# A float32 transpose on one core: four staggered column ranges, 32 KB store packets, two load slots, no seam

## The chip, the cores and the metric

The kernel runs on 1 core of a Trainium2 chip. The metric is device time in microseconds (us), lower is better.

## The reference

```python
x = np.random.randn(8192, 8192).astype(np.float32)     # 256 MiB

def reference(x):
    return np.transpose(x)
```

The kernel reads 268.4 MB and writes 268.4 MB of device memory. No arithmetic counts; the work is moving bytes.

## The kernel before

In what follows PE is the matrix engine (PEld its weight loads), ACT and DVE are the scalar and the vector engine, SPq is the queue that issues the DMAs, and PSUM is the memory that PE writes.

The matrix is cut into two strips of 4096 columns. A step loads a *chunk*: 128 rows of one strip, 16 KB per SBUF partition, 2 MB in all. PE transposes the 32 blocks of 128x128 against an identity matrix into PSUM, ACT and DVE copy them into *regions* in SBUF, and a region is stored when it has collected a *window* of 8 chunks. A region holds a *range* of 4 blocks (512 columns of the input, which are 512 rows of the output) by 8 chunks, so each stored output row is 8x128 floats, 4 KB long.

The eight ranges close their windows at successive steps, so one 2 MB store is issued at each step. This needs short windows (1 to 7 chunks, so rows of 512 B to 3.5 KB) at the start and the end of each strip.

```python
    S = 32; B = 4; W = 8; NR = S // B; NIN = 3; NREG = 9; NPS = 8     # one line each in the kernel
    ...
        for t, (s, c) in enumerate(chunks):               # 2 strips x 64 chunks
            nc.tensor.wait_ge(s_ld[t % NIN], 16 * (t // NIN + 1))
            closing = []
            for q in [(c + k) % NR for k in range(NR)]:
                if q not in window:
                    end = min(c + (q - c) % W, CH - 1)    # windows end one step apart, and at the strip's end
                    r = free.pop(0)
                    window[q] = (c, end, r)
                    ...                                   # copier waits until region r was stored
                ...                                       # 4 transposes, 1 copy into the region
            for q, e, count in closing:
                ...
                dst = out[j0:j0 + B * P, c0 * P:c0 * P + rows]
                dst = dst.rearrange("(b q) i -> q b i", q=P)
                nc.sync.wait_ge(s_cp[e], count)
                st = wide_dma(nc, nc.sync, "qSPDynamicHW", dst, regs[r][:, :B * rows])
                ...
            if t + NIN < len(chunks):                     # the next load, behind the stores
                nc.sync.wait_ge(s_pe, n)
                load(t + NIN)
```

`wide_dma` issues a store whose source is one contiguous run per partition, so that a DMA packet reads 16 KB of one partition (4 blocks) and writes four output rows of 4 KB.

Of the kernel before, what the change touches and what calls it, by code (L numbers as in the profile page):

```python
# [1 line left out]

# [4 lines left out]


def physical(ap):


    t = ap.tensor
    dims = [list(d) for d in ap.ap]
    if len(dims) == 2:
        dims.insert(1, [dims[1][1], 1])
    return mybir.PhysicalAccessPattern(
        ap=dims,
        offset=ap.offset,
        dtype=ap.dtype,
        memref=t.name,  # L20
        memsetref=t.name + "_set",
    )


def wide_dma(nc, eng, queue, out, in_):


    return eng.add_instruction(
        mybir.InstDMACopy(
            mode="Copy",  # L30
            name=nc.get_next_instruction_name(),
            engine=eng.engine,
            ins=[physical(in_)],
            outs=[physical(out)],
            queue=queue,
        )
    )


@with_exitstack  # L40
def kernel(
    ctx: ExitStack,
    tc: tile.TileContext,
    x: bass.AP,
    out: bass.AP,
):





    nc = tc.nc
    P = 128
    N, M = x.shape
    assert x.shape == out.shape[::-1]
    dt = x.dtype

    S = 32
    B = 4
    W = 8  # L60
    NR = S // B
    NIN = 3
    NREG = 9
    NPS = 8
    CH = N // P
    J = S * P

    with tc.tile_critical():  # L68
        nc.alloc_sbuf_tensor("pad", [P, 32], dt)
        ident = nc.alloc_sbuf_tensor("ident", [P, P], dt).ap()  # L70
        ins = [nc.alloc_sbuf_tensor(f"in{k}", [P, J], dt).ap() for k in range(NIN)]
        regs = [nc.alloc_sbuf_tensor(f"reg{k}", [P, B * W * P], dt).ap() for k in range(NREG)]
        pss = [nc.alloc_psum_tensor(f"ps{k}", [P, B * P], dt).ap() for k in range(NPS)]

        s_id = nc.alloc_semaphore("s_id")
        s_ld = [nc.alloc_semaphore(f"s_ld{k}") for k in range(NIN)]
        s_st = [nc.alloc_semaphore(f"s_st{k}") for k in range(NREG)]
        s_pe = nc.alloc_semaphore("s_pe")
        s_cp = [nc.alloc_semaphore("s_cpa"), nc.alloc_semaphore("s_cpv")]

        nc.gpsimd.memset(ident, 0.0).then_inc(s_id, 1)  # L81
        nc.gpsimd.wait_ge(s_id, 1)
        nc.gpsimd.affine_select(  # L83
            out=ident,
            in_=ident,
            compare_op=mybir.AluOpType.not_equal,
            fill=1.0,
            base=0,
            pattern=[[-1, P]],
            channel_multiplier=1,  # L90
        ).then_inc(s_id, 1)
        nc.tensor.wait_ge(s_id, 2)

        chunks = [(s, c) for s in range(M // J) for c in range(CH)]

        def load(t):
            s, c = chunks[t]
            nc.sync.dma_start(
                out=ins[t % NIN], in_=x[c * P:(c + 1) * P, s * J:(s + 1) * J]
            ).then_inc(s_ld[t % NIN], 16)  # L100

        for t in range(NIN):
            load(t)

        n = 0
        copied = [0, 0]
        bank = [None] * NPS
        free = list(range(NREG))
        stored = [0] * NREG
        window = {}  # L110
        stores = 0
        for t, (s, c) in enumerate(chunks):
            nc.tensor.wait_ge(s_ld[t % NIN], 16 * (t // NIN + 1))
            closing = []
            for q in [(c + k) % NR for k in range(NR)]:
                if q not in window:

                    end = min(c + (q - c) % W, CH - 1)
                    r = free.pop(0)
                    window[q] = (c, end, r)  # L120
                    if stored[r]:
                        (nc.scalar, nc.vector)[q % 2].wait_ge(s_st[r], 16 * stored[r])
                c0, end, r = window[q]
                rows = (end - c0 + 1) * P
                view = regs[r][:, :B * rows].rearrange("p (b i) -> p b i", b=B)
                ps = pss[n % NPS]
                e = q % 2
                if bank[n % NPS] is not None:
                    nc.tensor.wait_ge(*bank[n % NPS])
                for b in range(B):  # L130
                    last = nc.tensor.transpose(  # L131
                        ps[:, b * P:(b + 1) * P],
                        ins[t % NIN][:, (q * B + b) * P:(q * B + b + 1) * P],
                        ident,
                    )
                last.then_inc(s_pe, 1)
                n += 1
                o = view[:, :, (c - c0) * P:(c - c0 + 1) * P]
                i = ps.rearrange("p (b i) -> p b i", b=B)
                (nc.scalar, nc.vector)[e].wait_ge(s_pe, n)  # L140
                if e == 0:
                    cp = nc.scalar.copy(out=o, in_=i)  # L142
                else:
                    cp = nc.vector.tensor_copy(out=o, in_=i)  # L144
                cp.then_inc(s_cp[e], 1)
                copied[e] += 1
                bank[(n - 1) % NPS] = (s_cp[e], copied[e])
                if c == end:
                    closing.append((q, e, copied[e]))
            for q, e, count in closing:  # L150
                c0, end, r = window.pop(q)
                rows = (end - c0 + 1) * P
                j0 = s * J + q * B * P
                dst = out[j0:j0 + B * P, c0 * P:c0 * P + rows]
                dst = dst.rearrange("(b q) i -> q b i", q=P)
                nc.sync.wait_ge(s_cp[e], count)
                if stores:
                    st = wide_dma(nc, nc.sync, "qSPDynamicHW", dst, regs[r][:, :B * rows])
                else:
                    st = nc.sync.dma_start(  # L160
                        out=dst, in_=regs[r][:, :B * rows].rearrange("q (b i) -> q b i", b=B)
                    )
                st.then_inc(s_st[r], 16)
                stores += 1
                stored[r] += 1
                free.append(r)
            if t + NIN < len(chunks):
                nc.sync.wait_ge(s_pe, n)
                load(t + NIN)
        for r in range(NREG):  # L170
            nc.sync.wait_ge(s_st[r], 16 * stored[r])


# [1 line left out]
_INS = ['x']  # L175
_OUTS = [((8192, 8192), 'float32')]


# [23 lines left out]
```

## Time and profile before

1267.5 us (median of 3 runs, 1266.26 to 1268.18).

| | before |
|---|---|
| span of the profiled execution | 1265.1 us |
| PE / DVE / ACT busy | 57% / 28% / 24% |
| GB/s in most slices | 426 to 431 |
| load, issue to landing | 23.5 us |

Lines of the profile's page: the mean busy share of the 16 DMA engines in 40 slices of the span (tenths) and the rate; the share of the chain of waits by engine and by line; the costliest groups (busy us, mean ns of one, then idle time before them and what ended it); DMA issues with size and us from issue to landing.

```profile
DMA  9999999999999999999999999999999999999998
GB/s 380 418 428 427 428 429 428 427 428 428 426 428 429 426 428 430 429 428 428 428 417 428 428 427 428 431 429 429 429 428 428 430 428 430 429 429 429 428 428 353
...
DMA 78%; PE 20%; issue 0%; DVE 0%; ACT 0%; SPq 0%; ACTq 0%
...
L131 PE MATMUL ps<-ident,in 128*128 128x128 f32 x4096 | 722.6, 359 | 514.8 <-DMA in<-in_x_dram 499.7
...
in<-in_x_dram SPq DMA_DIRECT2D x128, 2048.0 KB, 23.5
out_dram<-reg SPq DMA_DIRECT2D x114, 2048.0 KB, 22.7
```

The DMA engines are busy all the time, the chain runs through them, and PE waits for loads. The Trainium skill, "DMA: Bandwidth & Descriptors", section "Where 436 GB/s comes from", gives 435.2 GB/s as the fabric's ceiling; this trace agrees with it as a ceiling, since the steady slices are at 428 to 429, 98.4% of it. (The same section says that for transfers between HBM, the device memory, and SBUF the memory side, at about 358 GB/s, binds. This trace, of one core, is above that, so the measurement decides.) So little is left to gain. The first, second, middle (seam) and last slices are slower.

The same in five uneven stretches (columns: stretch, its us, busy us of each engine with the number of instructions, granted PE clock, DMA share, GB/s):

```profile
0.00:70.00 70.00, 43.08 (x288) 41.69 (x288) 24.47 (x36) 22.18 (x37) 0.70 (x6) 0.88 0.98 402
70.00:590.00 520.00, 304.14 (x1696) 291.57 (x1696) 146.97 (x213) 124.18 (x212) 0.00 (x0) 0.74 1.01 428
590.00:740.00 150.00, 85.17 (x480) 79.26 (x480) 40.98 (x60) 34.85 (x60) 0.00 (x0) 0.70 1.01 426
740.00:1200.00 460.00, 268.28 (x1504) 257.14 (x1504) 130.04 (x188) 110.12 (x188) 0.00 (x0) 0.75 1.01 429
```

The fifth stretch is the rest of the span. The DMA share can pass 1 (it is 1.006 from 100 to 580 us), so the records of successive packets overlap in part.

### The profile page before, as it was taken

To read this page: it belongs to the slowest core of one execution; us is meant where nothing else is said; L and a number is where in the kernel's file an instruction comes from. 1 tells how busy PE (TensorE), PEld (TensorE's weight loads), DVE (VectorE), ACT (ScalarE), POOL (GpSimd) and SP (SyncE) were. 2 spreads that over 40 slices of the span, in tenths; PEclk is the share of its full clock that TensorE was granted. 3 is DMA by queue.
4 is the path that set the end of the run, shared out by engine and by line. 5 is a ranking of instruction groups with operands and counts; after the bars stand their busy time and mean duration, and the time that the engine had idled before them with its cause. 6 is when DMAs were issued, how large, how long until landed. Compare 5 with 4: busy or idle time off the path is not lost.

```text
span 1265.1 us, 9814 instructions
## 1 busy us (share of the span) xinstructions
PE 722.6 (57%) x4096; PEld 690.6 (55%) x4096; DVE 353.5 (28%) x512; ACT 300.7 (24%) x513; POOL 0.7 (0%) x6
## 2 busy tenths in 40 slices
PE   6555656665556555565456655656566555665651
PEld 6555645555456555564455555655455555565551
DVE  3322222322223222232133322223223222232220
ACT  3322222222222222222122222222222222222220
POOL 0000000000000000000000000000000000000000
PEclk8877686777776877768667777686867877777675
DMA  9999999999999999999999999999999999999998
GB/s 380 418 428 427 428 429 428 427 428 428 426 428 429 426 428 430 429 428 428 428 417 428 428 427 428 431 429 429 429 428 428 430 428 430 429 429 429 428 428 353
DMA packets 39308, 537.51 MB, mean 425 GB/s; under 512 B 4320, under 2 KB 4832, under 8 KB 6240
## 3 DMA queue, kind: packets, MB, share of 16 engines
q1 hardware_dynamic: 39264, 536.89, 100.0%
q8 instruction: 32, 0.52, 0.2%
q14 instruction: 12, 0.10, 0.0%
HBM read 268.44 MB, written 268.44 MB: 424 GB/s over the span
## 4 chain that ended last, share of the span: by engine, by line
DMA 78%; PE 20%; issue 0%; DVE 0%; ACT 0%; SPq 0%; ACTq 0%
DMA in<-in_x_dram 75%; PE ps L131 20%; DMA out_dram<-reg 2%; DVE reg L144 0%; ACT reg L142 0%; SPq L197 0%; SPq L68 0%; ACTq L140 0%
## 5 line engine op out<-in xcount | busy, mean ns | idle before, releaser
L131 PE MATMUL ps<-ident,in 128*128 128x128 f32 x4096 | 722.6, 359 | 514.8 <-DMA in<-in_x_dram 499.7
L131 PEld LDWEIGHTS ps<-ident,in 128*128 128x128 f32 x4096 | 690.6, 193 | 546.5 <-DMA in<-in_x_dram 520.8
L144 DVE COPY reg<-ps 128x512 f32<-128x512 f32 x512 | 353.5, 692 | 884.2 <-PE ps L131 850.8
L142 ACT COPY reg<-ps 128x512 f32<-128x512 f32 x512 | 299.4, 586 | 936.5 <-PE ps L131 902.7
L142 ACT ACT_TABLE_LOAD x1 | 1.3, 1283 | 0.9 <-SPq L68 0.9
L83 POOL TENSOR_SCALAR_AFFINE_SELECT ident<-ident 128x128 f32<-128x128 f32 x1 | 0.3, 292 | 0.2 <-POOL ident L81 0.2
L81 POOL MEMSET ident<- 128x128 f32 x1 | 0.2, 204 | 0.5 <-SPq L68 0.5
L186 POOL MEMSET const-bfloat16-1.0<- 128x1 bf16 x1 | 0.1, 101 | 0.0
L186 POOL MEMSET const-uint8-127<- 128x1 uint8 x1 | 0.1, 101 | 0.0
L186 POOL MEMSET const-float32-0.0<- 128x1 f32 x1 | 0.1, 98 | 0.2 <-issue 0.2
L186 POOL MEMSET const-float32-1.0<- 128x1 f32 x1 | 0.1, 98 | 0.0
## 6 DMA issues: line engine op xcount, KB each, us to landing
in<-in_x_dram SPq DMA_DIRECT2D x128, 2048.0 KB, 23.5
out_dram<-reg SPq DMA_DIRECT2D x114, 2048.0 KB, 22.7
out_dram<-reg SPq DMA_DIRECT2D x4, 1792.0 KB, 20.1
out_dram<-reg SPq DMA_DIRECT2D x4, 1536.0 KB, 19.2
out_dram<-reg SPq DMA_DIRECT2D x4, 1280.0 KB, 19.1
out_dram<-reg SPq DMA_DIRECT2D x4, 1024.0 KB, 17.9
out_dram<-reg SPq DMA_DIRECT2D x4, 768.0 KB, 16.3
out_dram<-reg SPq DMA_DIRECT2D x4, 512.0 KB, 13.2
```

What stands on the lines that cost most here:

```text
L81: nc.gpsimd.memset(ident, 0.0).then_inc(s_id, 1)
L83: nc.gpsimd.affine_select(out=ident, in_=ident, compare_op=mybir.AluOpType.not_equal, fill=1.0, base=0, pattern=[[-1, P]], channel_multipl ...
L131: last = nc.tensor.transpose(ps[:, b * P:(b + 1) * P], ins[t % NIN][:, (q * B + b) * P:(q * B + b + 1) * P], ident,)
L142: cp = nc.scalar.copy(out=o, in_=i)
L144: cp = nc.vector.tensor_copy(out=o, in_=i)
L186: nc = _bacc.Bacc("TRN2", target_bir_lowering=False, num_devices=1)
```

## The change

Its intent: halve the number of store packets (32 KB of SBUF each instead of 16), and remove the seam between the strips and the staircase of short windows there.

- Four ranges of 8 blocks, windows of 8 chunks, so a region is 32 KB per partition. Five regions (160 KB) leave room for two load slots instead of three.
- Range q begins 2q steps after range 0, and takes the rows of a strip round, so that it begins strip 1 while later ranges still finish strip 0. A load still is one contiguous piece of a row.
- A window that crosses the end of the rows or of the strip is stored in two or three parts. One window of 2 chunks per range opens the kernel; the last ones are 6 chunks.
- The load of two steps on is issued ahead of the stores of a step. PSUM copies are 128x1024 instead of 128x512.

```diff
-    S = 32
-    B = 4
+    B = 8
     W = 8
-    NR = S // B
-    NIN = 3
-    NREG = 9
-    NPS = 8
+    NR = 4
+    G = W // NR
+    NREG = 5
+    NPS = 4
...
+        at = [((t - G * q) // CH, q) for q in range(NR) if t >= G * q]
+        active.append(sorted(a for a in at if a[0] < NS))
...
+            while t1 + 1 < hi and t1 % W != (G * q + G - 1) % W:
+                t1 += 1
...
+                if t == t1 or (t + 1) % CH == 0 or (t + 1 - lo) % CH == 0:
+                    parts.append((a, t))
...
+    order = [("L", t) for t in range(4)]
+    order += [("S", 1), ("L", 4), ("S", 3), ("L", 5), ("L", 6), ("L", 7), ("S", 5)]
+    for t in range(6, T):
+        if t + 2 < T:
+            order.append(("L", t + 2))
+        if closing[t]:
+            order.append(("S", t))
...
+                for a, z in w["parts"]:
+                    rows = (z - a + 1) * P
...
+                    i0 = a % CH * P
+                    dst = out[j0:j0 + R, i0:i0 + rows].rearrange("(b q) i -> q b i", q=P)
...
+                    src = regs[w["reg"]][:, base:base + B * rows]
+                    if stores:
+                        st = wide_dma(nc, nc.sync, "qSPDynamicHW", dst, src)
```

More of the change, by code (lines that the diff above doesn't have):

```diff
@@ L56 @@
     dt = x.dtype
-    S = 32
-    B = 4
+    B = 8
     W = 8
-    NR = S // B
-    NIN = 3
-    NREG = 9
-    NPS = 8
+    NR = 4
+    G = W // NR
+    NREG = 5
+    NPS = 4
     CH = N // P
-    J = S * P
+    J = NR * B * P
+    NS = M // J
+    T = NS * CH + (NR - 1) * G
+    SPLIT = range(3 * G, 5 * G)
+    active = []
+    for t in range(T):
+        at = [((t - G * q) // CH, q) for q in range(NR) if t >= G * q]
+        active.append(sorted(a for a in at if a[0] < NS))
+    closing = [[] for _ in range(T)]
+    window_of = {}
+    for q in range(NR):
+        lo, hi = G * q, G * q + NS * CH
+        t0 = lo
+        while t0 < hi:
+            t1 = t0
+            while t1 + 1 < hi and t1 % W != (G * q + G - 1) % W:
+                t1 += 1
+            parts = []
+            a = t0
+            for t in range(t0, t1 + 1):
+                if t == t1 or (t + 1) % CH == 0 or (t + 1 - lo) % CH == 0:
+                    parts.append((a, t))
+                    a = t + 1
+            w = {"q": q, "t0": t0, "t1": t1, "parts": parts}
+            closing[t1].append(w)
+            for t in range(t0, t1 + 1):
+                window_of[t, q] = w
+            t0 = t1 + 1
+    EARLY = 3 * G
+    order = [("L", t) for t in range(4)]
[5 more added lines that the diff above has]
+            order.append(("S", t))
+    assert sorted(k for o, k in order if o == "L") == list(range(T))
+    assert sorted(k for o, k in order if o == "S") == [t for t in range(T) if closing[t]]
     with tc.tile_critical():
-        nc.alloc_sbuf_tensor("pad", [P, 32], dt)
         ident = nc.alloc_sbuf_tensor("ident", [P, P], dt).ap()
-        ins = [nc.alloc_sbuf_tensor(f"in{k}", [P, J], dt).ap() for k in range(NIN)]
+        ins = [nc.alloc_sbuf_tensor(f"in{k}", [P, J], dt).ap() for k in range(2)]
         regs = [nc.alloc_sbuf_tensor(f"reg{k}", [P, B * W * P], dt).ap() for k in range(NREG)]
@@ L75 @@
         s_id = nc.alloc_semaphore("s_id")
-        s_ld = [nc.alloc_semaphore(f"s_ld{k}") for k in range(NIN)]
+        s_ld = [nc.alloc_semaphore(f"s_ld{k}") for k in range(2)]
+        s_half = [nc.alloc_semaphore(f"s_half{k}") for k in range(2)]
+        s_early = [nc.alloc_semaphore(f"s_early{k}") for k in range(EARLY)]
         s_st = [nc.alloc_semaphore(f"s_st{k}") for k in range(NREG)]
@@ L79, with landed @@
         s_cp = [nc.alloc_semaphore("s_cpa"), nc.alloc_semaphore("s_cpv")]
+        copier = [nc.scalar, nc.vector]
+        R = B * P
+        home = []
+        pieces = []
+        count = {}
+        def landed(s):
+            count[s.name] = count.get(s.name, 0) + 16
+            return s, count[s.name]
+        last_use = []
+        for t in range(T):
+            n = len(active[t]) * R
+            if t < EARLY:
+                buf, off = [
+                    (ins[0], 0), (ins[0], R), (ins[0], 2 * R),
+                    (ins[1], 0), (regs[NREG - 1], 0), (regs[NREG - 1], 3 * R),
+                ][t]
+                home.append(buf[:, off:off + n])
+                pieces.append([(*landed(s_early[t]), 0, n)])
+                last_use.append(None)
+                continue
+            k = t % 2
+            home.append(ins[k][:, :n])
+            if t in SPLIT:
+                pieces.append([(*landed(s_half[k]), 0, n // 2), (*landed(s_ld[k]), n // 2, n)])
+            else:
+                pieces.append([(*landed(s_ld[k]), 0, n)])
+            last_use.append([2, 3][k] if t < EARLY + 2 else t - 2)
+        free = list(range(NREG))
+        stored = [0] * NREG
+        for t in range(T):
+            for s, q in active[t]:
+                w = window_of[t, q]
+                if w["t0"] == t:
+                    r = free.pop(0)
+                    w["reg"], w["before"] = r, stored[r]
+            for w in closing[t]:
+                stored[w["reg"]] += len(w["parts"])
+                free.append(w["reg"])
         nc.gpsimd.memset(ident, 0.0).then_inc(s_id, 1)
@@ L92 @@
         nc.tensor.wait_ge(s_id, 2)
-        chunks = [(s, c) for s in range(M // J) for c in range(CH)]
-        def load(t):
-            s, c = chunks[t]
-            nc.sync.dma_start(
-                out=ins[t % NIN], in_=x[c * P:(c + 1) * P, s * J:(s + 1) * J]
-            ).then_inc(s_ld[t % NIN], 16)
-        for t in range(NIN):
-            load(t)
         n = 0
+        done = []
         copied = [0, 0]
         bank = [None] * NPS
-        free = list(range(NREG))
-        stored = [0] * NREG
-        window = {}
-        stores = 0
-        for t, (s, c) in enumerate(chunks):
-            nc.tensor.wait_ge(s_ld[t % NIN], 16 * (t // NIN + 1))
-            closing = []
-            for q in [(c + k) % NR for k in range(NR)]:
-                if q not in window:
-                    end = min(c + (q - c) % W, CH - 1)
-                    r = free.pop(0)
-                    window[q] = (c, end, r)
-                    if stored[r]:
-                        (nc.scalar, nc.vector)[q % 2].wait_ge(s_st[r], 16 * stored[r])
-                c0, end, r = window[q]
-                rows = (end - c0 + 1) * P
-                view = regs[r][:, :B * rows].rearrange("p (b i) -> p b i", b=B)
+        for t in range(T):
+            todo = list(pieces[t])
+            for k, (s, q) in enumerate(active[t]):
+                if todo and todo[0][2] == k * R:
+                    nc.tensor.wait_ge(todo[0][0], todo[0][1])
+                    todo.pop(0)
+                w = window_of[t, q]
+                e = q % 2
                 ps = pss[n % NPS]
-                e = q % 2
                 if bank[n % NPS] is not None:
@@ L132 @@
                         ps[:, b * P:(b + 1) * P],
-                        ins[t % NIN][:, (q * B + b) * P:(q * B + b + 1) * P],
+                        home[t][:, k * R + b * P:k * R + (b + 1) * P],
                         ident,
@@ L137 @@
                 n += 1
-                o = view[:, :, (c - c0) * P:(c - c0 + 1) * P]
+                if w["t0"] == t and w["before"]:
+                    copier[e].wait_ge(s_st[w["reg"]], 16 * w["before"])
+                copier[e].wait_ge(s_pe, n)
+                a, z = next(p for p in w["parts"] if p[0] <= t <= p[1])
+                base = (a - w["t0"]) * R
+                o = regs[w["reg"]][:, base:base + (z - a + 1) * R]
+                o = o.rearrange("p (b i) -> p b i", b=B)[:, :, (t - a) * P:(t - a + 1) * P]
                 i = ps.rearrange("p (b i) -> p b i", b=B)
-                (nc.scalar, nc.vector)[e].wait_ge(s_pe, n)
                 if e == 0:
@@ L147 @@
                 bank[(n - 1) % NPS] = (s_cp[e], copied[e])
-                if c == end:
-                    closing.append((q, e, copied[e]))
-            for q, e, count in closing:
-                c0, end, r = window.pop(q)
-                rows = (end - c0 + 1) * P
-                j0 = s * J + q * B * P
-                dst = out[j0:j0 + B * P, c0 * P:c0 * P + rows]
-                dst = dst.rearrange("(b q) i -> q b i", q=P)
-                nc.sync.wait_ge(s_cp[e], count)
-                if stores:
-                    st = wide_dma(nc, nc.sync, "qSPDynamicHW", dst, regs[r][:, :B * rows])
-                else:
-                    st = nc.sync.dma_start(
-                        out=dst, in_=regs[r][:, :B * rows].rearrange("q (b i) -> q b i", b=B)
-                    )
-                st.then_inc(s_st[r], 16)
-                stores += 1
-                stored[r] += 1
-                free.append(r)
@@ L167 @@
-            if t + NIN < len(chunks):
-                nc.sync.wait_ge(s_pe, n)
-                load(t + NIN)
+                if w["t1"] == t:
+                    w["copied"] = (s_cp[e], copied[e])
+            assert not todo
+            done.append(n)
+        stores = 0
+        for what, t in order:
+            if what == "L":
+                if last_use[t] is not None:
+                    nc.sync.wait_ge(s_pe, done[last_use[t]])
+                s, q = active[t][0]
+                j0 = s * J + q * R
+                i0 = t % CH * P
+                for sem, _, a, z in pieces[t]:
+                    nc.sync.dma_start(
+                        out=home[t][:, a:z], in_=x[i0:i0 + P, j0 + a:j0 + z]
+                    ).then_inc(sem, 16)
+                continue
+            for w in closing[t]:
+                nc.sync.wait_ge(*w["copied"])
+                for a, z in w["parts"]:
+                    rows = (z - a + 1) * P
+                    j0 = (a - G * w["q"]) // CH * J + w["q"] * R
+                    i0 = a % CH * P
+                    dst = out[j0:j0 + R, i0:i0 + rows].rearrange("(b q) i -> q b i", q=P)
+                    base = (a - w["t0"]) * R
+                    src = regs[w["reg"]][:, base:base + B * rows]
+                    if stores:
+                        st = wide_dma(nc, nc.sync, "qSPDynamicHW", dst, src)
+                    else:
+                        st = nc.sync.dma_start(
+                            out=dst, in_=src.rearrange("q (b i) -> q b i", b=B)
+                        )
+                    st.then_inc(s_st[w["reg"]], 16)
+                    stores += 1
```

## The prediction

> **What bounds the kernel now.** The DMA engines. The page's slices show DMA at 9 tenths or more everywhere and 426 to 431 GB/s in almost every slice (380 first, 418 second, 417 at the seam between the strips, 353 last). PE is busy 57%, ACT 24%, DVE 28%. The chain of waits is 78% DMA, 20% PE; loads take 23.5 us from issue to landing, mostly queueing, since 2 MB need 4.9 us at 428 GB/s. The Trainium skill, "DMA: Bandwidth & Descriptors", section "Where 436 GB/s comes from", gives 435.2 GB/s as the ceiling of the 16 ports. 536.87 MB at that rate take 1233.6 us (estimate); the kernel takes 1267.5. So at most 34 us (2.7%) can be had.
>
> **Where those 34 us are,** from the trace's DMA packet records:
> - A 16 KB packet takes 611 or 616 ns (mean 615), 4 KB 165, 8 KB 315, 12 KB 466: about 75.2 ns per 2 KB plus 9 to 14 ns per packet. With 2,160 data packets per engine, the per-packet part is roughly 25 us.
> - The first packet starts at 2.0 us; one load's 16 semaphore increments spread over 3 us at first, 6 us at the end. The slowest engine sets the time.
> - Start and seam (staircase of short stores, a dip to 380 GB/s) lose 1 to 2 us each.
>
> **What the change does.**
> 1. Stores read 32 KB of SBUF per packet instead of 16. 142 store DMAs of 8 packets per engine become about 76: 528 packets per engine fewer, at 12 ns: -6.3 us.
> 2. Loads: 128 become about 138, 80 more packets per engine at 9 ns: +0.7 us. Fewer semaphore packets (9 ns each): -0.5 us.
> 3. No seam staircase: -1.5 us. The copies' waits for free regions there (33 us on DVE, 32 on ACT) go too, but queued stores hid them.
> 4. Start: small loads, four early 1 MB stores of 1 KB pieces; perhaps a gap of 1 to 2 us near 10 us, when the first 3 MB of loads have run out and the first store waits for cold transposes (32 took 6.5 us in the first step of before). Net +0.5.
> 5. End: the last stores are 3 MB; the engines' spread stays: 0.
> 6. Two load slots, five regions: a load waits for PE two steps earlier. A step of 2 MB in and 2 MB out is 9.8 us of DMA; its 32 transposes take 3.5 to 6.5 us. By the queue order, with 2 us from last byte to PE, each load is issued 4 us or more before the queue would run dry. No loss in steady state.
> 7. Half as many copies of twice the size: ACT and DVE are off the path.
>
> Only what shortens the DMA stream (1 to 4) is on the critical path: together -7.1 us.
>
> **Predicted: 1260.0 us (-0.6%), 8 in 10 between 1254 and 1267.** Faster by over 2%: 0.02 (needs under 1242 us, within 1% of the ceiling). Within 2%: 0.95. Slower: 0.03.
>
> **What would show it.** Store packets of 32 KB at 1215 to 1220 ns (at twice 616, step 1 is wrong). Steady slices at 430 to 432 GB/s. No low slice in the middle. PE still waiting for loads; load issue to landing only 9 to 14 us, with DMA still at 9 tenths.
>
> **What would make it wrong.** Two load slots too few when the granted clock drops (0.75 on average now): DMA gaps each second step. The spread between engines exceeding the shallower queue, so that engines idle. Writes of eight 4 KB rows per packet, 4 MB apart, stalling where four did not. A longer start-up gap.

## The result

The changed kernel takes 1277.59 us (median of 4 runs, 1276.54 to 1277.95), the kernel before 1267.84 us in the same rounds: a ratio of 1.0078 (95% interval 1.006 to 1.0095), 0.8% slower. It is correct. Ratios here are the mean time of one kernel's fast runs over that of the other's of the same rounds, so not quite the ratio of the medians quoted.

The page of the changed kernel, the same lines, with the store issues by size:

```profile
DMA  9999999999999999999999999999999999999998
GB/s 341 417 421 436 425 428 434 424 430 433 426 431 430 425 432 424 430 431 421 410 386 425 421 425 433 423 431 430 427 430 430 426 431 423 427 431 424 429 423 323
...
DMA 69%; PE 30%; issue 0%; DVE 0%; SPq 0%
...
L205 PE MATMUL ps<-ident,in 128*128 128x128 f32 x4048 | 593.5, 321 | 649.4 <-DMA in<-in_x_dram 649.4
...
in<-in_x_dram SPq DMA_DIRECT2D x118, 2048.0 KB, 14.4
out_dram<-reg SPq DMA_DIRECT2D x56, 4096.0 KB, 24.4
...
out_dram<-reg SPq DMA_DIRECT2D x12, 1024.0 KB, 18.7
out_dram<-reg SPq DMA_DIRECT2D x4, 3072.0 KB, 20.4
out_dram<-reg SPq DMA_DIRECT2D x4, 2048.0 KB, 18.2
```

```profile
0.00:70.00 70.00, 43.14 (x288) 40.69 (x288) 18.76 (x16) 21.44 (x21) 0.70 (x6) 0.85 0.98 383
70.00:590.00 520.00, 243.93 (x1664) 237.64 (x1664) 128.20 (x105) 105.31 (x104) 0.00 (x0) 0.72 1.00 429
590.00:740.00 150.00, 70.44 (x494) 68.52 (x495) 36.74 (x30) 30.77 (x31) 0.00 (x0) 0.74 1.00 413
740.00:1200.00 460.00, 217.87 (x1493) 212.15 (x1490) 115.11 (x94) 94.77 (x94) 0.00 (x0) 0.72 1.00 427
```

The loads wait less in the queue (14.4 us instead of 23.5) and DMA is still at 9 tenths. The steady stretches are unchanged, 427 to 429 GB/s; the start (402 to 383) and the seam (426 to 413) are worse, although the DMA share there is still 0.98 to 1.00. So the engines did not idle there: their packets took longer.

The start shows it most, here from 10 to 25 us, before and changed:

```profile
10.00:25.00 15.00, 11.81 (x90) 11.57 (x88) 8.21 (x12) 6.35 (x12) 0.00 (x0) 0.98 1.02 404
10.00:25.00 15.00, 7.65 (x50) 7.17 (x48) 3.67 (x3) 3.70 (x4) 0.00 (x0) 0.77 0.99 323
```

To add this up I use one measure throughout. *Lost time* of a stretch is its length less the bytes moved in it over 428.4 GB/s (about the rate of the steady stretches), with the bytes from the trace's DMA packet records, each packet's bytes spread evenly over its duration. All bytes at 428.4 GB/s would take 1253.2 us; the lost times add up to the span less that.

| stretch, us | before | changed | changed, again |
|---|---|---|---|
| 0-70 (start) | 4.7 | 8.3 | 9.0 |
| 70-590 | 0.9 | 0.1 | 0.0 |
| 590-740 (seam) | 1.1 | 5.8 | 4.8 |
| 740-1200 | -0.2 | 0.9 | 0.2 |
| 1200-end | 5.4 | 7.7 | 8.0 |
| sum | 11.9 | 22.8 | 22.0 |

The difference of the spans, 10.9 us, is at the start (+3.6), the seam (+4.7) and the end (+2.3). The middle gave 0.7 us in the first strip and took 1.1 in the second. "Changed, again" is the profile of a later run (below); differences of up to 1.5 us between stretches of two profiles of the same kernel are noise (such pairs of all kernels run twice differ by as much).

### The profile page after: what moved, and what is told of

Its sections match the earlier page's. It is cut to its first block, busy times and chain, and to the rows that moved or that the text cites. A ratio compares the mean times of both kernels' runs of the same rounds, so it can differ in the third digit from the quotient of the medians.

```text
span 1276.0 us, 9182 instructions
## 1 busy us (share of the span) xinstructions
PE 602.5 (47%) x4096; PEld 585.0 (46%) x4096; DVE 313.4 (25%) x256; ACT 260.4 (20%) x257; POOL 0.7 (0%) x6
## 4 chain that ended last, share of the span: by engine, by line
DMA 69%; PE 30%; issue 0%; DVE 0%; SPq 0%
DMA in<-in_x_dram 68%; PE ps L205 30%; DMA reg<-in_x_dram 1%; DVE reg L223 0%; SPq L28 0%; SPq L290 0%; SPq L115 0%
## 5 line engine op out<-in xcount | busy, mean ns | idle before, releaser
L205 PE MATMUL ps<-ident,in 128*128 128x128 f32 x4048 | 593.5, 321 | 649.4 <-DMA in<-in_x_dram 649.4
L205 PEld LDWEIGHTS ps<-ident,in 128*128 128x128 f32 x4048 | 576.4, 170 | 666.0 <-DMA in<-in_x_dram 661.1
L223 DVE COPY reg<-ps 128x1024 f32<-128x1024 f32 x256 | 313.4, 1225 | 949.5 <-PE ps L205 949.5
L221 ACT COPY reg<-ps 128x1024 f32<-128x1024 f32 x256 | 259.1, 1012 | 991.9 <-PE ps L205 991.9
L205 PE MATMUL ps<-ident,reg 128*128 128x128 f32 x48 | 9.1, 375 | 9.8 <-DMA reg<-in_x_dram 9.8
L205 PEld LDWEIGHTS ps<-ident,reg 128*128 128x128 f32 x48 | 8.6, 204 | 10.3 <-DMA reg<-in_x_dram 10.3
## 6 DMA issues: line engine op xcount, KB each, us to landing
in<-in_x_dram SPq DMA_DIRECT2D x118, 2048.0 KB, 14.4
```

The source lines that it names most:

```text
L205: last = nc.tensor.transpose(ps[:, b * P:(b + 1) * P], home[t][:, k * R + b * P:k * R + (b + 1) * P], ident,)
L221: cp = nc.scalar.copy(out=o, in_=i)
L223: cp = nc.vector.tensor_copy(out=o, in_=i)
```

## The experiments

Three theories of the loss. A: the short stores at start, seam and end (20 of them of 2 to 6 chunks, whose output rows are 1 to 3 KB) make the engines slow. B: the shallow queue of two load slots does. R, on the expected gain: a packet's fixed cost goes by the output rows that it writes, not by packets.

### 16 KB store packets in the changed kernel (store16)

```diff
-                    src = regs[w["reg"]][:, base:base + B * rows]
+                    H = B // 2
+                    for h in range(2):
+                        j1 = j0 + h * H * P
+                        dst = out[j1:j1 + H * P, i0:i0 + rows].rearrange("(b q) i -> q b i", q=P)
+                        src = regs[w["reg"]][:, base + h * H * rows:base + (h + 1) * H * rows]
```

> The changed kernel, with each store of a region issued as two DMAs that read 16 KB of SBUF per packet (blocks 0-3, then 4-7), four 4 KB rows per packet as before the change. Theory P (the prediction's step 1: about 12 ns per packet): about 528 packets per engine more, so 6 us slower than the changed kernel, near 1283 us. Theory R (the cost goes by written rows of 4 KB, not by packets): 16 KB store packets at 611 to 616 ns again, two of them worth one 32 KB packet of 1228 ns, so within 1.5 us of the changed kernel's 1277.6 us.

1278.72 us (1277.73 to 1281.7), 1.1 us from the changed kernel's median, though in other rounds; the ratios to before, 1.0090 (1.0062 to 1.0117) and 1.0078 (1.0060 to 1.0095), show no difference. The packet records of 100 to 580 us have 16 KB packets at 611 and 616 ns again. Halving the store packets again costs nothing to speak of: R, not the prediction's step 1.

### Eight and sixteen rows per packet in the kernel before (before_b8w4, before_b16w2)

Store packets and stores keep their size (16 KB, 2 MB, one per step); only the rows are shorter and more.

```diff
-    B = 4
-    W = 8
+    B = 8      # second kernel: 16
+    W = 4      # second kernel: 2
-    NPS = 8
+    NPS = 4    # second kernel: 2
```

> The kernel before with four ranges of 8 blocks and windows of 4 chunks: stores still read 16 KB of SBUF per packet and are 2 MB each, one per step, but a packet writes eight rows of 2 KB instead of four of 4 KB. Theory R (cost by written row): store packets near 622 to 627 ns instead of 611 to 616, 5 to 10 us slower, 1273 to 1278 us. Theory P (cost by packet): 611 to 616 ns, within 2 us of 1267.8 us.

> The kernel before with two ranges of 16 blocks and windows of 2 chunks: stores are still 2 MB, one per step, 16 KB of SBUF per packet, but each packet writes sixteen rows of 1 KB, in the steady state too. If 1 KB rows at a 32 KB pitch stall the engines by themselves: steady rate far below 428 GB/s (under 400), over 40 us slower. If they cost only the per-row term (2.5 ns each): store packets near 645 ns, 418 GB/s, about 15 to 20 us slower, 1283 to 1290 us, and the dips of the changed kernel need another reason.

1284.48 us (ratio 1.0132, 1.0111 to 1.0153) with eight rows: more than expected. Start, seam and end lose 10 us more than before, the steady stretches 7 us more; that the first is due to the still shorter rows of its staircase is likely but not tested. 1747.44 us (ratio 1.378) with sixteen. The packet records of the steady state (100 to 580 us) give the usual durations. They don't tell a 16 KB store packet from a 16 KB load packet; in the changed kernel, where only loads have that size, 98% take 611 ns, so the other frequent duration is taken as the store's.

| store packet | rows it writes | usual ns | over bytes/27.2 |
|---|---|---|---|
| 16 KB, before | 4 of 4 KB | 616 (about four in ten 611) | 13.6 |
| 16 KB, four ranges | 8 of 2 KB | 626 | 23.6 |
| 16 KB, two ranges | 16 of 1 KB | 645 | 42.6 |
| 32 KB, changed | 8 of 4 KB | 1228 (some 1213) | 23.3 |

27.2 bytes per ns is 435.2 GB/s over 16 engines. The surplus goes by rows, about 2.5 ns each plus some 4 ns per packet, at 16 KB and at 32 KB alike. That is R. A 32 KB packet of 1228 ns replaces two of 616: 4 ns saved, at most 2 us over the 448 such packets per engine (56 stores of 8 each). The Trainium skill, "DMA: Bandwidth & Descriptors", section "Why small descriptors are slow (HBM only)", has a fixed overhead of a few cycles per packet and 32 bytes of metadata per DMA operation; these runs agree that there is a small fixed cost, and put it at the written row.

The two-range kernel shows more. Half of its 16 KB packets take 645 ns or less, but their mean is 834 ns: with rows of 1 KB in every store the packets stall, and some loads among them (39% of all packets take 620 ns or less, and half of all are loads), with DMA still busy:

```profile
70.00:590.00 520.00, 219.98 (x1216) 210.96 (x1216) 87.08 (x38) 70.95 (x38) 0.00 (x0) 0.69 0.98 309
```

309 GB/s instead of 428. Stores of 1 KB rows are slow beyond the per-row cost, in an order and a queue depth that were fine with 4 KB rows.

### Long rows in the changed kernel (longruns, long_seam)

The short stores read the same region bytes at the same time, but write them as fewer rows of 4 KB, to a wrong place. The very first store, issued the ordinary way, is left alone. `long_seam` does it at the seam only.

```diff
+                    k = z - a + 1
+                    if k < W and stores:                  # long_seam: if k < W and 40 <= a < 100:
+                        i0 = i0 // R * R
+                        dst = out[j0:j0 + k * P, i0:i0 + R].rearrange("(b q) i -> q b i", q=P)
```

> Wrong result on purpose: the changed kernel, with every store of fewer than 8 chunks (at start, seam and end; all but the very first) written as rows of 4 KB instead of rows of 1 to 3 KB, the same bytes, order, waits and loads; only the place in the output is wrong. Theory A (short output rows stall the DMA engines at start, seam and end): the dips to 255-390 GB/s go, about 6 to 9 us faster, 1269 to 1272 us. Theory B (the shallow queue of two load slots, or the shorter loads, lose the time there): no change, within 2 us of 1277.6 us, dips stay.

> Wrong result on purpose: the changed kernel with 4 KB rows for the short stores of the seam alone; start and end as changed. Theory A (short rows): 4 to 5.5 us faster than the changed kernel's 1277.6 us, 1272 to 1274 us, with the loss between 590 and 740 us down from 5.8 to about 1 us and start and end as before. The rival (seam loss from the wrapped, split loads or the shallow queue): no change, 1276 us or more.

All short stores with long rows: 1271.35 us. The seam alone: 1276.96 us, much less than expected, in rounds in which the kernel before scattered too (1267.7 to 1272.9). So both were run again beside the changed kernel, in the same rounds, on one chip.

> The changed kernel once more, as the yardstick for the three that follow on the same chip: 1276.5 to 1278.5 us, with 5 to 6.5 us lost between 590 and 740 us.

> Wrong result on purpose, as the first time. In its profile the seam's loss fell from 5.8 to 0.8 us, but the timed median only by 0.6 us, in rounds whose kernel before also scattered (1267.7 to 1272.9 us), and about 2 us more was lost after the seam. Theory A, all of it returned: 4 us or more below the changed kernel of the same rounds. Theory A with a give-back (stalls between 740 and 1200 us that come in this kernel where the seam is not slowed): 1 to 3 us below, with the loss from 740 to 1200 us again near 3 us. Rival: no difference.

> Wrong result on purpose, as the first time: all short stores but the first in 4 KB rows. Again 5 to 7 us below the changed kernel of the same rounds.

| same rounds | median, us | range | ratio to before | start | seam | 740-1200 | end |
|---|---|---|---|---|---|---|---|
| changed | 1277.13 | 1276.82 to 1277.96 | 1.0080 | 9.0 | 4.8 | 0.2 | 8.0 |
| long rows at seam | 1275.88 | 1274.74 to 1277.49 | 1.0069 | 9.3 | 0.3 | 3.2 | 8.4 |
| long rows everywhere | 1271.99 | 1271.52 to 1273.14 | 1.0039 | 6.9 | 1.0 | 3.4 | 7.1 |

(The last four columns are lost time by the profile.) The seam and the second strip with long rows at the seam:

```profile
590.00:740.00 150.00, 74.66 (x512) 72.77 (x512) 39.18 (x32) 32.40 (x32) 0.00 (x0) 0.74 1.01 428
740.00:1200.00 460.00, 214.19 (x1472) 208.66 (x1472) 112.64 (x92) 93.21 (x92) 0.00 (x0) 0.72 1.00 426
```

Nothing but the rows of the short stores differs (their length, their number and their place in the output), and the seam goes from 413-415 GB/s to 428. So at the seam theory A holds: the wrapped and split loads and the two slots are the same. The kernel before writes short rows at its seam too, but only 1.5 MB in rows of 1 KB or less, against 6 MB here. The smaller number of rows is worth about 1 us of the gain, at 2.5 ns for each (an estimate); the rest is stalls that the longer rows don't have.

But of the 4.5 us won there the measured time shows 1.3 (the ranges of the two kernels overlap), because about 3 us more are lost in the second strip; this came in all four profiles of the two long-row kernels (2.8 to 3.4 us against 0.2 and 0.9).

It is tempting to say that the changed kernel catches up after its slow seam, and that the other two lose what they won because the seam was not slowed. The record does not bear that out. The store16 and pitch28 kernels have a slow seam (5.4 and 5.7 us lost), and they lose 3.2 and 4.5 us in the second strip as well. The landings of the loads in slot 0 don't decide it either. From the 34th to the 61st refill of the slot (54 steps) the last of the 16 engines took 529.5 and 529.8 us in the two profiles of the changed kernel, against 531.2 and 532.5 with long rows at the seam; but one refill earlier (33rd to 60th) it took 532.0 and 531.8 against 531.9 and 532.9. At the first strip's pace (432.4 us for 44 steps) 54 steps are 530.7 us. So why the second strip is slower in these kernels stays open.

In sum, the rows cost 5.1 us in the same rounds (6.2 by the first runs). Most of it came back with start and end, 3.9 us more than with the seam alone. That is half of what the change lost: with long rows everywhere the kernel is still 5.3 us above the kernel before, and its profile has this at the start (6.9 us lost against 4.7), at the end (7.1 against 5.4) and in the second strip (3.4 against -0.2).

### Short rows at another pitch (pitch28)

Its output is wrong, which doesn't matter for the time.

```diff
+                    if z - a + 1 < W and stores and z < 2 * CH - 16:
+                        dst = SimpleNamespace(tensor=out.tensor, dtype=dt,
+                            offset=out.offset + j0 * N + i0 % 1024,
+                            ap=[[N - 1024, P], [P * N, B], [1, rows]])
```

> Wrong result on purpose: the changed kernel, with the short stores of start and seam (not the first store, not the end) keeping their rows of 1 to 3 KB and their number, but with the rows of neighbouring partitions 28 KB apart in the output instead of 32 KB. Theory A1 (a short row is slow in itself): no change against the changed kernel, 1277.6 us within 2 us, dips at start and seam stay. Theory A2 (many short rows at the same place of a power-of-two pitch collide in the memory): the dips go as with long rows; about 5 us faster, near 1272 us, and the loss between 590 and 740 us falls from 5.8 to about 1 us.

1280.53 us (ratio 1.0095), seam loss 5.7 us, start 9.0 us: no gain. The Trainium skill, "DMA: Bandwidth & Descriptors", section "Latency and other measured facts", reports slow copies at row pitches of large powers of two, from 512 KiB to 8 MiB, and that 4 KiB more cured the pitch of 4 MiB. Moving neighbouring rows from 32 KB to 28 KB apart did not cure the stalls here, so that pitch is not their cause. The eight rows of one packet stayed 4 MB apart, which is one of the page's slow pitches; this run does not test it. Rows of 4 KB at the same 4 MB run at 428 GB/s in the kernel before, so the distance alone is not enough.

### Two load slots in the kernel before (before_nin2)

```diff
-    NIN = 3
+    NIN = 2
```

> The kernel before with two load slots instead of three, nothing else. Theory A (short rows): slots hardly matter as the regions hold enough queued work; within 2 us of 1267.8 us. Theory B (shallow queue): 5 us or more slower, 1273 us or more, with DMA activity below 16 engines in the middle.

1277.74 us (ratio 1.0076), 10.3 us slower than before. Theory A alone falls. But the loss is of another kind: the engines idle, at start and seam only. Ten us at the seam, and the first strip:

```profile
650.00:660.00 10.00, 9.51 (x64) 9.27 (x62) 5.23 (x8) 4.59 (x8) 0.00 (x0) 0.75 0.60 226
70.00:590.00 520.00, 304.05 (x1696) 291.48 (x1696) 146.64 (x212) 124.17 (x212) 0.00 (x0) 0.75 1.01 429
```

The DMA share is 0.60 where the kernel before has 1.00 in the same 10 us. Lost time is 9.0 us at the start and 8.0 us at the seam, and 0.4 and 0.5 us in the steady stretches. In the changed kernel the DMA share at the seam is 1.00, so it has two slots without this idling. The next experiments show what pays for that.

### The change without its order (before_b8w8, b8w8_loadfirst)

Four ranges, 32 KB packets, two slots and five regions, but the strips one after the other with all ranges at the same rows, as before.

```diff
-    B = 4
+    B = 8
-    NIN = 3
-    NREG = 9
-    NPS = 8
+    NIN = 2
+    NREG = 5
+    NPS = 4
-            for q in [(c + k) % NR for k in range(NR)]:
+            for q in [(c // 2 + k) % NR for k in range(NR)]:
-                    end = min(c + (q - c) % W, CH - 1)
+                    end = min(c + (2 * q + 1 - c) % W, CH - 1)
```

> Part of the change alone: four ranges of 8 blocks, 32 KB of SBUF per store packet, two load slots, five regions, in the strip order of before (all ranges at the same rows, windows closing two steps apart, a staircase at start and seam, full 2 MB loads from the start). My theory: two load slots and only one spare region leave engines idle at start and seam as two slots did in the kernel before, where it cost 10 us; here 10 to 25 us slower than before, 1278 to 1293 us, steady state at 428 GB/s. So the staggered order of the change would be what pays for two slots. The rival, that the stagger brings nothing and all the loss comes from short rows, expects 1272 us or less, since this has fewer short stores.

1362.24 us (ratio 1.0737): 94 us, far more than the 10 to 25 expected, and in the steady state, not only at start and seam. Who holds up the queue's own issuing (waited-for engine and line; us in total, times, longest):

```profile
SPq L28 <- DVE reg L144: 450.3, 34, 17.4
SPq L28 <- ACT reg L142: 429.4, 34, 15.6
SPq L98 <- PE ps L131: 353.4, 124, 12.6
```

The queue stands 880 us at stores (line 28), waiting for the copies. The kernel of before issues a step's load behind its stores, so the loads behind it wait too. The second kernel moves three lines:

```diff
+            if t + NIN < len(chunks):
+                nc.sync.wait_ge(s_pe, n)
+                load(t + NIN)
             for q, e, count in closing:
 ...
-            if t + NIN < len(chunks):
-                nc.sync.wait_ge(s_pe, n)
-                load(t + NIN)
```

> The last experiment (four ranges, 32 KB store packets, two slots, five regions, strip order of before; 1362 us) with one change: in each step the load of two steps on is issued ahead of the closing stores, as the changed kernel does, not behind them. Theory Q (behind a 4 MB store, the next load leaves only one load in the queue while PE and copies prepare the next store, so the queue runs dry every two steps): idle engines in the steady state go, 50 us or more faster, 1275 to 1300 us, with loss left at start and seam. If the 94 us came from the 32 KB packets or four-range windows themselves, it stays above 1340 us.

1280.73 us (ratio 1.0087): 81 us back. Waits and rate now:

```profile
SPq L98 <- PE ps L131: 1116.2, 126, 16.0
SPq L28 <- DVE reg L144: 18.3, 2, 17.7
```

```profile
70.00:590.00 520.00, 248.00 (x1689) 241.60 (x1690) 128.33 (x105) 106.33 (x105) 0.00 (x0) 0.72 1.01 429
0.00:70.00 70.00, 38.44 (x256) 36.81 (x256) 19.60 (x16) 17.48 (x17) 0.70 (x6) 0.88 0.93 347
590.00:740.00 150.00, 73.68 (x490) 70.25 (x488) 38.15 (x32) 31.30 (x31) 0.00 (x0) 0.73 0.99 403
```

So with 4 MB stores, loads ahead of stores are what makes two slots enough in the steady state. (With 2 MB stores the kernel before with two slots lost nothing there, with its loads behind them.) This kernel differs from the changed one in its order and in the smaller first loads that go with it: it loses 13.7 us at the start, 9.1 at the seam and 5.0 at the end, where the changed kernel loses 8.3, 5.8 and 7.7. By the profiles the stagger helps at start and seam, and costs 2 to 3 us at the end; in the measured time (ratios 1.0087 and 1.0078) the two kernels can't be told apart. Its 32 KB packets also bring no steady gain to speak of: -0.4 us lost in each strip, against 0.9 and -0.2 before.

### Fewer short stores, correct (fullwin)

Each range counts its windows from its own first step. The 2-chunk stores of the start go; the seam has two stores each of 2, 4 and 6 chunks instead of six, two and two.

```diff
-            while t1 + 1 < hi and t1 % W != (G * q + G - 1) % W:
+            while t1 + 1 < hi and (t1 + 1 - lo) % W:
...
-    order += [("S", 1), ("L", 4), ("S", 3), ("L", 5), ("L", 6), ("L", 7), ("S", 5)]
+    order += [("L", 4), ("L", 5), ("L", 6), ("L", 7)]
```

> Correct result: the changed kernel with each range's windows counted from that range's own first step, so that no window of 2 chunks opens at the start, the first store comes after step 7, and the seam has two stores each of 2, 4 and 6 chunks instead of six of 2, two of 4 and two of 6. Theory A: the seam's loss falls from 5.8 to 2 to 3 us, about 3 us faster there. At the start the short stores are gone, but loads alone wait for PE with two slots: idle engines (activity under 16) between 15 and 40 us, costing 3 to 6 us more than the short stores did. In sum 1276 to 1281 us, no better than the changed kernel.

> Correct result, as the first time: 5 to 6.5 us below the changed kernel of the same rounds, and still 2 to 5 us above the kernel before.

1271.90 us, and 1272.30 us (1270.82 to 1273.34) in the later rounds, where the changed kernel had 1277.13: 4.8 us faster, a little less than expected, and correct. The second profile:

```profile
0.00:70.00 70.00, 40.44 (x288) 37.40 (x288) 19.59 (x16) 21.44 (x21) 0.70 (x6) 0.86 0.98 398
30.00:40.00 10.00, 7.16 (x60) 6.21 (x58) 4.94 (x5) 4.05 (x4) 0.00 (x0) 1.00 0.98 331
590.00:740.00 150.00, 71.62 (x500) 69.72 (x498) 38.28 (x32) 32.42 (x32) 0.00 (x0) 0.73 1.00 422
```

The seam loses 1.8 us (3.2 in the first profile) as theory A expects. My expectation for the start was wrong: I expected idle engines to cost more than the short stores did, but the start loses 5.4 us instead of 9.0. The second line shows that short rows are not all there is to the start: from 30 to 40 us, with no row under 4 KB being stored, loads in 8 KB packets took 390 ns on average, where they took 314 in the 10 us before. This kernel is the best version of this shape that I ran, and still slower than the kernel before (ratio 1.0038, 1.0025 to 1.0050; in the first rounds 1.0016, 0.9993 to 1.0039).

No version here beats the kernel before. Two things were not run: a third load slot in the changed kernel, and loads that give each range its own rows, which would spare the short stores at the seam.

### The end of the changed kernel, by its trace

In order of time (start us, us, engine, what; idle time before in brackets):

```profile
1246.71 6.46 PE L205 MATMUL ps<-ident,in 128*128 128x128 f32 x32 [15.42 <-DMA in<-in_x_dram]
...
1250.42 3.12 SPq L242 DMA_DIRECT2D in<-in_x_dram  x2
...
1253.59 9.86 SPq L28 DMA_DIRECT2D out_dram<-reg  x3
1257.94 3.27 PEld L205 LDWEIGHTS ps<-ident,in 128*128 128x128 f32 x16 [5.00 <-DMA in<-in_x_dram]
```

```profile
1250.00:1255.00 5.00, 3.18 (x18) 2.94 (x16) 2.45 (x2) 1.01 (x1) 0.00 (x0) 0.76 0.75 220
```

The last two loads wait for PE's work on the load of two steps before, and the store behind them waits as well, so the queue runs low: the DMA share is 0.75 for 5 us, about 1.3 us of idle engines. So here theory B is right as far as the trace tells; no run tests it. Long rows took only 0.9 us off the end in the same rounds (8.0 to 7.1), which is within the noise of such a stretch.

## Why the prediction was wrong

What bounds the kernel was right: the DMA stream decides, and DMA stays at 9 tenths. No run passed the ceiling on any gain. The measured time is 17.6 us above the predicted one because four terms of the sum failed, in steps 1, 3, 4 and 5.

- **Step 1, "528 packets per engine fewer, at 12 ns: -6.3 us".** The count was right: 76 store DMAs. The 12 ns were not a cost per packet. Every wide store packet in the records of before wrote four rows, whatever its size, so their intercept could not tell a packet's cost from that of its rows. The runs show about 2.5 ns per row, and a 32 KB packet at 1228 ns where I wrote 1215 to 1220 (and that at twice 616, or 1232, the step is wrong): 4 ns saved, not 12. Undoing the step cost 1.1 us, within the noise. At most 2 us were there, and the steady rate did not show even that.
- **Step 3, "No seam staircase: -1.5 us".** It became +4.7 us in the profile, and the seam of the kernel before had only 1.1 us to give. The wrapped rows leave ten short stores there instead of a staircase, six of them with rows of 1 KB, and long rows in their place took the seam's loss from 4.8 to 0.3 us. I saw the parts in the code and priced only their packets, not their rows. About 3 of the 4.5 us did not show in the total time: as much was lost in the second strip, and why stays open.
- **Step 4, "Net +0.5" at the start.** +3.6 us. I looked for idle engines near 10 us. There is little of that; from 10 to 25 us the DMA share is 0.99 at 323 GB/s, where before had 404. Packets were slow once the stores of 1 KB rows began. About 0.9 us of it (an estimate) is the first store, issued the ordinary way as 1,024 packets of 1 KB: they took 3.5 us of the 16 engines' time where their bytes need 2.4, and the smaller first store of before 0.9 where its bytes need 0.6. Leaving those stores out (the fullwin kernel) took the start from 9.0 to 5.4 us in the same rounds; long rows, with the first store left as it is, took it to 6.9.
- **Step 5, "the engines' spread stays: 0" at the end.** +2.3 us. The queue runs low when the loads shrink, 1.3 us of it idle engines.
- **Step 6, two slots without loss in the steady state.** Right: 427 to 429 GB/s. Two slots alone cost 10 us in the kernel before, and the new shape without its issue order 94 us; the change had that in hand.
- **Step 2 and step 7** were right as far as can be seen: about 138 load DMAs, and ACT and DVE off the chain.
- Of what I named as able to make it wrong, the longer start-up came, but not as a gap. Eight rows per packet 4 MB apart did not stall in the steady state (32 KB packets at 1228 ns).

What stays open: why rows of 1 KB stall the engines (it is not the 32 KB pitch of neighbouring rows, and the two-range kernel shows it in the order of before; the 4 MB between the rows of a packet is not tested with short rows), why loads are slow at the start of fullwin without them, and why the second strip loses about 3 us in several kernels.

## What to carry to other kernels

When a cost is read off the packets of one kernel, look at what all those packets share before it is called a cost per packet: here each wrote four rows, and the rows were most of the cost. A schedule that removes a seam by cutting windows can pay for it in short output rows; count the stores by row length at the edges, for at 1 KB they cost more than their bytes here. And with few load slots and large stores, issue the next load ahead of a store that must wait.

## What the Trainium skill lacked or had wrong

- "DMA: Bandwidth & Descriptors", section "Specifications", has 512 B as the smallest transfer for line rate. With all stores in rows of 1 KB (at a 32 KB pitch, mixed with 16 KB loads) this core moved 309 GB/s instead of 428. The page has no figure of Trainium2 for stores of 1 KB rows.
- The same page, section "Why small descriptors are slow (HBM only)", gives the fixed cost in cycles and bytes, without a figure in ns. These runs put it at about 2.5 ns for each row that a store packet writes, plus some 4 ns per packet, at packets of 16 and 32 KB.
- The same page, section "Latency and other measured facts", has no row pitch under 512 KiB. Here, changing the pitch of short rows from 32 to 28 KB gained nothing (1280.5 us against 1277.6 us).
- No page I read has a number for how far the 16 engines drift apart within one stream: in the kernel before, the increments of the first load came within 0.3 us and those of the last loads within 6 us, so the slowest engine ends several us after the fastest. (The 3 us "at first" of the prediction are the spread some loads later.)
